# Output projection of a hybrid attention and retention block in seven half-size products

## Chip, cores and metric

One Trainium2 chip; the kernel runs on one core. The metric is device time in microseconds, the median of the runs of a kernel. The engines are named as the profile names them: PE is the Tensor engine (PEld its weight loads), DVE the Vector engine, ACT the Scalar engine, POOL GpSimd, SP the Sync engine, whose queue issues nearly all DMAs of this kernel.

## The reference

A block over 1024 tokens of width 2048, float32. One input projection (2048 to 5632 columns) feeds windowed attention (16 heads of 64, 4 key and value heads, a bias per head and distance, a sink) and bidirectional retention (8 heads, 64 keys, 128 values), each with a gate; the two branches are put side by side and go through the output projection, a residual and a last norm:

```python
h = rmsnorm(x, norm_w)
q_a, k_a, v_a, g_a, q_r, k_r, v_r, g_r = split(h @ w_in)
attn = rmsnorm(windowed_attention(q_a, k_a, v_a, sink, rel_bias), attn_out_norm_w) * silu(g_a)
ret = head_groupnorm(bidirectional_retention(rotary(q_r), rotary(k_r) / 8, v_r, ...), ret_gn_w) * silu(g_r)
mixed = concatenate([attn, ret], -1)          # 1024 x 2048
out = rmsnorm(x + mixed @ w_out, final_norm_w)
```

## The kernel before

Every operand of the two large projections is held as two float32r parts, high and low (`split`: a cast on ACT, then a subtraction on DVE or POOL), and a product is three matmuls: high by high, high by low, low by high.

Input projection: 22 units of 256 columns (`UNITS`), each over 16 rows of 128 of K (`k`), 8 weight tiles of 128 x 512 per unit. Normalised input lies in `hT`, 32 rows of 1024. Unit by unit the result is evicted (`evac`). The order of units is written out: keys, values and the first gates, then gates (`ga` of attention, `gr` of retention) between queries (`qa`), then pairs of `qk` and `vr` for retention, then the last gate (`gr`, 3).

Attention and retention run as generators beside the units: after each group of matmuls `point()` is called, which pumps one step of `jobs` (an attention job for each of four head groups g, later a retention job for each of four head pairs) at a pace per job, and at every second point one step of `aux` (gate post-processing, rotary, norms, bias rows, decay tables). `drain` runs a queue on until something is done. Each engine runs its own instructions in the order that the program comes to have; SP is one such queue for DMAs, and a DMA that waits there holds the ones behind it.

Weights: `w_load(i)` fetches the raw tile `wr` two tiles ahead, `w_split(i)` makes `wh` and `wl` one tile ahead. Raw tiles have two buffers; `wh` and `wl` have two each, and four once retention is over (`wide`). The subtraction is on POOL for the input weights and on DVE for the output weights.

An attention step takes 128 queries of a head: two matmuls of scores into `psS`, a DVE operation that adds the bias and finds the maximum (`P`, `nmx`), an exponential on ACT (L454), the normalisation on DVE (L462), transposes on PE into the one bank `psT` (L502), the copy of these to `PTh` on ACT (L513) and `PTl` on DVE, and the product with the values into `psO`.

Bias: `bias_rows` makes one row of 512 per head and copies it to 128 partitions through SBUF to the DRAM tensor `bd`, 16 heads in a row, a load `t<-br` and a store `bd<-t` each. Gates: `gate_post` takes a tanh on ACT (L362) and a multiply-add on DVE and stores to `gd`. Branch outputs go to the DRAM tensor `md`.

Output projection: two token halves (`hf`) by four column blocks of 512 (`cb`), each over 16 rows of K by four token blocks of 128, so 12 matmuls per weight tile. `mixed_row` fetches a row of `md`, multiplies in norms and gates where these are still missing, and splits it into `hT`: the first half during the last unit, the second during the first units of the projection. Banks `psM` and the set `psS`, `psT`, `psO` take turns. The last column block of the second half goes token block by token block, 48 matmuls each, from weights that were split ahead (on POOL).

## Time and profile before

| | us |
|---|---|
| median of 3 runs | 1580.43 (1579.05 to 1583.06) |
| profiled execution | 1581.46 |
| its span, first to last instruction | 1579.7 |
| mean granted TensorE clock | 0.994 of full speed |
| busy: PE | 1539.7 (97%) |
| busy: DVE | 798.9 (51%) |
| busy: ACT | 525.2 (33%) |
| busy: POOL | 414.1 (26%) |
| DMA, mean | 109 GB/s |

The stages in the profiled span: input units and setup to about 225 us, attention beside input units to about 800 us, retention beside input units to about 1240 us, the output projection from there. A busy time counts the time in which an engine has an instruction under way; matmuls overlap, so a busy PE is not one at its peak rate. An idle time is given with what ended it. A row of a group reads: line, engine, operation, output<-input by name, shapes, count, then busy us and mean ns of one, then the idle time just before these and what ended most of it.

### The profile page before, as it was taken

How to read it: one execution, taken by the hardware profiler on the slowest of the kernel's cores; microseconds unless marked ns; L12 is line 12 of the kernel's file. 1: busy time of each engine (PE TensorE's matmuls, PEld its weight loads, DVE VectorE, ACT ScalarE, POOL GpSimd, SP SyncE). 2: the span in 40 equal slices, each digit the busy share in tenths (PEclk: the TensorE clock that was granted, in tenths of full speed). 3: DMA queues.
4: the chain of work that ended last, by engine and by line, in shares of the span. 5: the costliest groups of instructions: out<-in, count | busy, mean ns of one | idle time of the engine just before them, and what ended most of it. 6: DMA issues, size and time to landing. Idle time of an engine off the chain costs nothing.

```text
span 1579.7 us, 22620 instructions
## 1 busy us (share of the span) xinstructions
PE 1539.7 (97%) x8338; PEld 1327.6 (84%) x8338; DVE 798.9 (51%) x1888; ACT 525.2 (33%) x1186; POOL 414.1 (26%) x435
## 2 busy tenths in 40 slices
PE   8979999999999999999999999999999999999997
PEld 6968888888888888888998998998988888888886
DVE  5511156644656478466534825735567463463323
ACT  5412145543554356456410111111123243433310
POOL 2212223332334334334331423323322000320000
PEclk9989999999999999999999999999999999999999
DMA  8774313131213123212231321312222565675423
GB/s 299 246 248 125 104 43 92 51 114 45 84 56 114 48 60 94 73 48 83 54 113 41 107 61 50 111 41 67 88 89 91 186 205 151 180 247 139 127 61 113
DMA packets 111020, 171.76 MB, mean 109 GB/s; under 512 B 17932, under 2 KB 39436, under 8 KB 110781
## 3 DMA queue, kind: packets, MB, share of 16 engines
q1 hardware_dynamic: 110908, 170.32, 35.3%
q8 instruction: 65, 1.06, 0.3%
q14 instruction: 47, 0.38, 0.1%
HBM read 138.26 MB, written 32.01 MB: 108 GB/s over the span
## 4 chain that ended last, share of the span: by engine, by line
PE 82%; DVE 8%; DMA 4%; issue 3%; ACT 1%; POOL 1%; SPq 0%; POOLq 0%; ACTq 0%; DVEq 0%
PE psM L817 14%; PE psM L818 14%; PE psM L819 14%; PE psM L811 3%; PE psM L812 3%; PE psM L810 3%; PE psM L900 3%; PE psM L901 3%; PE psM L899 3%; PE psT L502 2%; DMA t<-br 1%; DVE t L102 1%; PE psS L900 1%; PE psS L899 1%; PE psS L901 1%
## 5 line engine op out<-in xcount | busy, mean ns | idle before, releaser
L817 PE MATMUL psM<-hT,wh 128*128 128x512 f32 x1088 | 443.0, 407 | 14.9 <-ACT t L741 8.7
L819 PE MATMUL psM<-hT,wl 128*128 128x512 f32 x1088 | 425.9, 392 | 2.0 <-POOL wl L99 2.0
L818 PE MATMUL psM<-hT,wh 128*128 128x512 f32 x1088 | 426.2, 392 | 0.0
L99 POOL TENSOR_TENSOR wl<-wr,wh 128x512 fp32r<-128x512 f32 x176 | 234.5, 1333 | 583.7 <-ACT wh L105 570.7
L105 ACT CAST wh<-wr 128x512 fp32r<-128x512 f32 x288 | 178.5, 620 | 568.7 <-PE psM L818 226.4
L817 PEld LDWEIGHTS psM<-hT,wh 128*128 128x128 f32 x1088 | 205.7, 189 | 53.6 <-ACT t L741 8.9
L819 PEld LDWEIGHTS psM<-hT,wl 128*128 128x128 f32 x1088 | 204.9, 188 | 47.3 <-POOL wl L99 2.4
L818 PEld LDWEIGHTS psM<-hT,wh 128*128 128x128 f32 x1088 | 206.1, 189 | 37.5 <-DVE hT L102 0.7
L810 PE MATMUL psM<-wh,hT 128*128 128x256 f32 x640 | 183.5, 287 | 1.4 <-ACT wh L105 1.4
L811 PE MATMUL psM<-wl,hT 128*128 128x256 f32 x640 | 181.9, 284 | 2.4 <-POOL wl L99 2.4
L812 PE MATMUL psM<-wh,hT 128*128 128x256 f32 x640 | 181.8, 284 | 0.0
L99 DVE TENSOR_TENSOR wl<-wr,wh 128x512 fp32r<-128x512 f32 x112 | 84.1, 751 | 130.8 <-ACT wh L105 130.7
L811 PEld LDWEIGHTS psM<-wl,hT 128*128 128x128 f32 x640 | 123.4, 193 | 3.0 <-POOL wl L99 2.8
L810 PEld LDWEIGHTS psM<-wh,hT 128*128 128x128 f32 x640 | 123.5, 193 | 2.5 <-ACT wh L105 1.6
L812 PEld LDWEIGHTS psM<-wh,hT 128*128 128x128 f32 x640 | 123.4, 193 | 0.0
L450 DVE CUSTOM_DVE_ANT_0 P<-psS,bias,nsink 128x384 f32<-128x384 f32 (+1 forms) x128 | 74.3, 580 | 91.7 <-PE psS L444 91.3
L454 ACT ACTIVATE P<-P,nmx 128x384 f32<-128x384 f32 (+1 forms) x128 | 75.6, 590 | 92.1 <-DVE nmx L450 90.7
L900 PE MATMUL psM<-wl,hT 128*128 128x512 f32 x256 | 100.0, 391 | 0.6 <-DVE wl L99 0.5
L899 PE MATMUL psM<-wh,hT 128*128 128x512 f32 x256 | 100.0, 391 | 0.0
L901 PE MATMUL psM<-wh,hT 128*128 128x512 f32 x256 | 99.7, 389 | 0.0
L99 POOL TENSOR_TENSOR acc<-acc,sq 64x128 f32<-64x128 f32 x112 | 54.9, 490 | 156.2 <-ACT sq L483 148.1
L99 DVE TENSOR_TENSOR t<-psM,rb 128x512 f32<-128x512 f32 x64 | 42.2, 685 | 93.4 <-PE psM L819 93.2
(200 smaller groups left out, 2259.6 us busy)
## 6 DMA issues: line engine op xcount, KB each, us to landing
wr<-in_w_in SPq DMA_DIRECT2D x176, 256.0 KB, 2.7
wr<-in_w_out SPq DMA_DIRECT2D x112, 256.0 KB, 2.8
t<-in_x SPq DMA_DIRECT2D x16, 512.0 KB, 6.9
mr<-md SPq DMA_DIRECT2D x32, 256.0 KB, 3.0
xr<-in_x SPq DMA_DIRECT2D x32, 256.0 KB, 3.9
out<-y SPq DMA_DIRECT2D x32, 256.0 KB, 3.0
t<-in_xT SPq DMA_DIRECT2D x15, 512.0 KB, 5.8
gd<-t SPq DMA_DIRECT2D x28, 256.0 KB, 2.4
```

The lines of the kernel that those rows point to most:

```text
L99: eng.tensor_tensor(o, x, y, op)
L105: A.copy(o_hi, x)
L454: A.activation(x[:, :W], x[:, :W], AF.Exp, bias=nmx[:, c : c + 1], scale=-1.0, accum_out=sums[:, c : c + 1])
L810: T.matmul(po, hh[:, sl], wh[:, ws], start=first and z == 0, stop=False, skip_group_check=True)
L811: T.matmul(po, hh[:, sl], wl[:, ws], start=False, stop=False, skip_group_check=True)
L812: T.matmul(po, hl[:, sl], wh[:, ws], start=False, stop=last, skip_group_check=True)
L817: T.matmul(p, wh[:, ws], hh[:, sl], start=first, stop=False)
L818: T.matmul(p, wh[:, ws], hl[:, sl], start=False, stop=False)
L819: T.matmul(p, wl[:, ws], hh[:, sl], start=False, stop=last)
L899: T.matmul(p, mh, wh, start=(k == 0), stop=False)
L900: T.matmul(p, mh, wl, start=False, stop=False)
L901: T.matmul(p, ml, wh, start=False, stop=(k == NK - 1))
```

## The change

The output projection is cut into four problems: the two halves of K (f = 0 is the attention half, f = 1 the retention half) by the two halves of the columns (u). Each is a product of 1024 x 1024 by 1024 x 1024, taken as 2 x 2 blocks of 512 and computed in seven products of blocks (Strassen, in Winograd's form) in place of eight. A product p takes 4 rows of K by 4 token blocks by 3 matmuls. Its right operand is a block of `w_out` or one of four differences of blocks; its left operand a block of `mixed` or one of four combinations.

- `w_combine(f)` makes the weight differences: per f, u and row j, five loads, four DVE subtractions and four stores to DRAM (`wd`). It runs from a third queue, `slow`, which `point()` pumps at two of three points (at every point once retention is over), beside attention.
- `weigh_rows` multiplies attention's 16 half rows by norm weight and norm, DRAM to DRAM, and `combine_rows(f, j)` makes four combinations per j (two loads, one DVE operation, one store to `cd`), both beside retention, on two buffers `wc`. The last (f = 1, j = 3) and `gate_rows` follow in the first products.
- All 28 rows of the first half of K are loaded and split during the last unit (two per k); the 28 of the second half while the products run.
- PSUM: sums of products are read while they still grow (product 0 alone, then 0 + 2, and so on); each product's banks are evicted by an addition to one of four output blocks, 112 evictions of 128 x 512 in place of 32. The first seven products use one bank set, the others two in turn. Output sums of u = 1 go to DRAM (`yd`) and back between the halves of K.
- The weights' subtraction is on POOL for f = 0 and on DVE for f = 1.
- Bias rows: copies are made per group of four heads, from `slow`, one head at a time on the two `wc` buffers; groups 0 and 1 come in the first units, 2 and 3 later beside attention.
- Gates: one Silu on ACT, no DVE operation, and the factor 0.5 that went with tanh is dropped from `ew`.
- `t2` has four buffers in place of six. Keys and values are fetched straight into the tiles in which they are split.
- The last product goes token block by token block, 12 matmuls each; norms and stores of the second half of tokens follow block by block.

```diff
+ORDERS = {(0, 0): (1, 0, 2, 4, 5, 3, 6), (1, 1): (0, 1, 2, 3, 6, 4, 5)}
+W_OUT = [(f, u, p, j) for f in range(2) for u in range(2)
+    for p in ORDERS.get((f, u), (0, 1, 2, 3, 4, 6, 5)) for j in range(4)]
...
-            split(hi, lo, r, G if i < W_IN_TILES else V)
+            split(hi, lo, r, V if i >= W_IN_TILES and W_OUT[i - W_IN_TILES][0] else G)
+    def w_combine(f):
+        for u in range(2):
+            for j in range(4):
+                x, y = wc_(), wc_()
+                SP.dma_start(x, quarter(f, u, j, 1))
+                SP.dma_start(y, quarter(f, u, j, 0))
+                yield from pause(3)
+                tt(V, y, x, y, ALU.subtract)
+                yield
+                SP.dma_start(wd[f, u, 1, j], y)
...
+        if pt[0] % 3 or wide[0] is not None:
+            pump(slow, 1)
...
-        for h in range(16 + 1):
-            if h < 16:
-                reps[h] = t2()
-                b0 = br[h : h + 1, 0:512]
-                SP.dma_start(reps[h], bass.AP(tensor=b0.tensor, offset=b0.offset, ap=[[0, 128], [1, 512]]))
-            if h:
-                SP.dma_start(bd[h - 1], reps.pop(h - 1))
-            yield
+    def bias_copies(g):
+        for h in range(4 * g, 4 * g + 4):
+            r = wc_()
+            b0 = br[h : h + 1, 0:512]
+            SP.dma_start(r, bass.AP(tensor=b0.tensor, offset=b0.offset, ap=[[0, 128], [1, 512]]))
+            yield from pause(4)
+            SP.dma_start(bd[h], r)
+            yield
...
-            e = t2()
-            A.activation(e, g, AF.Tanh, scale=0.5)
-            yield
-            stt(V, g, e, 1.0, g, ALU.add, ALU.mult)
+            A.activation(g, g, AF.Silu)
+            yield
...
+    def combine_rows(f, j, tile):
+        if f:
+            yield lambda: ("ret", j) in done
+        for n, (x0, x1, op) in enumerate((
+            (q_mix(f, j, 2), q_mix(f, j, 3), ALU.add),
+            (q_mix(f, j, 0), q_mix(f, j, 2), ALU.subtract),
+            (cd[f, 1, j], q_mix(f, j, 0), ALU.subtract),
+            (q_mix(f, j, 1), cd[f, 0, j], ALU.subtract),
+        )):
+            x, y = tile(), tile()
+            SP.dma_start(x, x0)
+            SP.dma_start(y, x1)
+            yield from pause(3)
+            tt(V, y, x, y, op)
+            yield
+            SP.dma_start(cd[f, (1, 2, 0, 3)[n], j], y)
+            yield from pause(2 if n < 2 else 4)
...
+    slow.append((bias_rows(), 16))
+    slow.append((bias_copies(0), None))
+    slow.append((bias_copies(1), None))
+    slow.append((w_combine(0), None))
+    slow.append((bias_copies(2), None))
+    slow.append((bias_copies(3), None))
+    slow.append((w_combine(1), None))
+    def weighed():
+        yield lambda: "attn_norm" in done
+        yield from weigh_rows()
+        for j in range(4):
+            yield from combine_rows(0, j, wc_)
+    slow.append((weighed(), None))
+    for j in range(3):
+        slow.append((combine_rows(1, j, wc_), None))
...
+    into = {0: (0,), 1: (0,), 2: (1,), 3: (3,), 4: (3,), 5: (2,), 6: (1,)}
+    for n in range(nprod):
+        f, u, p, _ = W_OUT[4 * n]
+        if n < 7:
+            if p in (0, 1, 3):
+                X = Y = [psum("M", 4) for _ in range(4)]
+        elif p == 0:
+            sets = ([psum("M", 4) for _ in range(4)], [pS(), pS(), pT(), pO()])
+            X, Y = sets if (2 * f + u) % 2 == 0 else sets[::-1]
+        banks = Y if p in (1, 3, 6) else X
...
+        def products(j, t):
+            wh, wl = wsp[W_IN_TILES + 4 * n + j]
+            hh, hl = (H[p][:, j, 512 * z + 128 * t : 512 * z + 128 * t + 128] for z in range(2))
+            fresh = j == 0 and p in (0, 1, 3)
+            T.matmul(banks[t], hh, wh, start=fresh, stop=False, skip_group_check=True)
+            T.matmul(banks[t], hh, wl, start=False, stop=False, skip_group_check=True)
+            T.matmul(banks[t], hl, wh, start=False, stop=(j == 3), skip_group_check=True)
```

Three places in the order of instructions. First ACT, beside the second attention job, around the four gate operations of unit `ga` 2 (L362 before, L432 now; the exponentials are L454 before, L516 now). Before:

```order
L362 ACTIVATE t_501_3904<-t_478_3818 128x512
L479 COPY sq_3883<-psO_3875 64x256
L513 CAST PTh_3895<-psT_3891 128x3x128
L362 ACTIVATE t_505_3938<-t_482_3841 128x512
L454 ACTIVATE P_3872,sums_3870<-P_3872,nmx_3869 128x384
L483 ACTIVATE sq_3883<-u_3882 64x256
L362 ACTIVATE t_519_4000<-t_483_3846 128x512
L362 ACTIVATE t_520_4016<-t_484_3851 128x512
L513 CAST PTh_3895<-psT_3932 128x3x128
L454 ACTIVATE P_3923,sums_3870<-P_3923,nmx_3869 128x384
```

Now:

```order
L432 ACT_TABLE_LOAD
L432 ACTIVATE t_514_3994<-t_514_3994 128x512
L545 ACTIVATE sq_4036<-u_4035 64x256
L516 ACT_TABLE_LOAD
L516 ACTIVATE P_4076,sums_4023<-P_4076,nmx_4022 128x384
L519 ACTIVATE esk_4024<-esk_4024 128x2
L575 CAST PTh_4048<-psT_4085 128x3x128
L127 CAST wh_4103<-wr_4014 128x512
L432 ACT_TABLE_LOAD
L432 ACTIVATE t_515_3999<-t_515_3999 128x512
L516 ACT_TABLE_LOAD
L516 ACTIVATE P_4121,sums_4119<-P_4121,nmx_4118 128x256
```

Each gate operation now has a table load ahead of it, and so has the next exponential; 44 table loads stand in the program in place of one. Next SP, in unit 1, where the bias copies begin (`br` is the row of a head, `bd` its copy on 128 partitions). Before:

```order
L253 DMA t_58_774<-br 128x512
L255 DMA bd<-t_55_724 128x512
L255 DMA bd<-t_56_738 128x512
L255 DMA bd<-t_57_759 128x512
L253 DMA t_59_789<-br 128x512
L255 DMA bd<-t_58_774 128x512
L253 DMA t_60_804<-br 128x512
L143 DMA wr_811<-in_w_in 128x512
L255 DMA bd<-t_59_789 128x512
```

Now:

```order
L325 DMA wc_655<-br 128x512
L365 DMA dc_718<-in_ret_decay_bwd 64x4x1
L370 DMA jc_725<-in_jcol 128x2
L325 DMA wc_733<-br 128x512
L327 DMA bd<-wc_655 128x512
L172 DMA wr_804<-in_w_in 128x512
L425 DMA kd<-t_34_462 128x512
L327 DMA bd<-wc_733 128x512
L325 DMA wc_821<-br 128x512
L172 DMA wr_875<-in_w_in 128x512
L397 DMA t_66_819<-in_masks 128x512
L325 DMA wc_894<-br 128x512
```

Fewer copies stand between two weight loads, on two buffers in place of six, and key stores and the decay masks stand between them. Last SP beside retention (`wr` are weights, `so` and `md` retention's own rows, L803, L804 and L808 the combinations). Before:

```order
L143 DMA wr_10744<-in_w_in 128x512
L661 DMA md<-so_10676 128x512
L552 DMA qd_11424<-qdd 128x256
L656 DMA so_10971<-gd 128x512
L143 DMA wr_10805<-in_w_in 128x512
L661 DMA md<-so_10787 128x512
L550 DMA dt_11422<-dd 128x2x128
L143 DMA wr_10881<-in_w_in 128x512
```

Now:

```order
L808 DMA cd<-wc_10114 128x512
L172 DMA wr_10156<-in_w_in 128x512
L803 DMA wc_10201<-md 128x512
L804 DMA wc_10202<-cd 128x512
L172 DMA wr_10223<-in_w_in 128x512
L808 DMA cd<-wc_10202 128x512
L723 DMA md<-so_10166 128x512
L803 DMA wc_10327<-md 128x512
L612 DMA dt_10823<-dd 128x2x128
L804 DMA wc_10328<-md 128x512
L718 DMA so_10524<-gd 128x512
L808 DMA cd<-wc_10328 128x512
```

Between two weight loads there is now a combination's store, which waits for DVE, and the next one's loads, of which the second waits for that store.

More of the change, by code (lines that the diff above doesn't have):

```diff
@@ L855, in hybrid_block @@
             drain(aux, ("ga", i))
+            drain(slow, ("bias", i))
             jobs.append((attn_job(i, st, 16 * u + 17), None))
@@ new lines, in hybrid_block, with y_block, y_tile, e_load @@
+    for r in range(28):
+        if r in staged:
+            c_split(r)
+    E = {}
+    squares, yrows = {}, {}
+    def y_block(u, e, t):
+        tok, c0 = 512 * (e // 2) + 128 * t, 1024 * u + 512 * (e % 2)
+        return slice(tok, tok + 128), slice(c0, c0 + 512)
+    def y_tile():
+        return outp[0].tile([128, 512], F32, tag="yb", name=nm("yb"), bufs=8)
+    def e_load(f, u, e):
+        while stores:
+            SP.dma_start(*stores.popleft()[1:])
+        if f and not u:
+            return
+        if not f and not u:
+            if e == 0:
+                yrows[0] = hp.tile([128, 8, 512], F32, tag="h7", name="h7f", bufs=1)
+            elif e == 1:
+                pass
+            elif 1 not in yrows:
+                yrows[1] = outp[0].tile([128, 8, 512], F32, name="ya")
+        if f and e >= 2:
+            yrows[e] = h4(e - 2, F32)
+        for t in range(4):
+            if f and e >= 2:
+                d = yrows[e][:, t, 0:512]
+            elif u:
+                d = y_tile()
+            else:
+                d = yrows[e // 2][:, 4 * (e % 2) + t, :]
+            rows, cols = y_block(u, e, t)
+            SP.dma_start(d, yd[4 * e + t] if f else a["x"][rows, cols])
+            E[u, e, t] = d
@@ new lines, in hybrid_block, with finish @@
+    stores = deque()
+    weigh = deque()
+    def finish(e2, t):
+        v = small(1, "fv", 2)
+        V.tensor_reduce(v, squares[4 * e2 + t], mybir.AxisListType.X, ALU.add)
+        V.tensor_scalar(v, v, 1.0 / D, EPS, ALU.mult, ALU.add)
+        y, w = rsqrt_small(v, 1, "f", 2)
+        tt(V, y, y, w, ALU.mult)
+        for u, e in ((0, 2 * e2), (0, 2 * e2 + 1), (1, 2 * e2), (1, 2 * e2 + 1)):
+            d = E[u, e, t]
+            rows, cols = y_block(u, e, t)
+            if not u or e == 3:
+                A.activation(d, d, AF.Copy, scale=y)
+            else:
+                stt(V, d, d, y, fw[:, cols], ALU.mult, ALU.mult)
+            SP.dma_start(out[rows, cols], d)
```

440 lines of the change are left out of this document (259 added, 181 removed).

## Prediction

> **What bounds the kernel now.** I read the page first, then busy time by stretches, the groups of instructions, the Tensor engine's idle times, and the Scalar and Sync engines in order of time.
>
> ```profile
> span 1579.7 us, 22620 instructions
> PE 1539.7 (97%) x8338; PEld 1327.6 (84%) x8338; DVE 798.9 (51%) x1888; ACT 525.2 (33%) x1186; POOL 414.1 (26%) x435
> ```
>
> Stretches (length, then busy us and count of PE, PEld, DVE, ACT, POOL, granted clock, DMA share, GB/s) of attention and of the output projection:
>
> ```profile
> 300.00:500.00 200.00, 197.56 (x997) 167.81 (x996) 113.85 (x289) 93.41 (x242) 72.81 (x90) 1.00 0.28 81
> 500.00:700.00 200.00, 196.90 (x998) 165.35 (x997) 121.08 (x311) 98.60 (x261) 74.19 (x95) 1.00 0.24 66
> 1300.00:1400.00 100.00, 100.00 (x443) 82.70 (x442) 42.76 (x61) 41.25 (x79) 21.18 (x17) 1.00 0.58 172
> ```
>
> TensorE sets the end: in the projection it is never idle, in attention it idles under 2%. So matmuls removed are time removed, and whatever makes TensorE wait is time added. A matmul's own duration is not its price:
>
> ```profile
> L899 PE MATMUL psM<-wh,hT 128*128 128x512 f32 x256 | 100.0, 391 | 0.0
> L899 PE MATMUL psS<-wh,hT 128*128 128x512 f32 x96 | 37.4, 389 | 0.0
> L899 PE MATMUL psT<-wh,hT 128*128 128x512 f32 x48 | 18.7, 389 | 0.0
> L899 PE MATMUL psO<-wh,hT 128*128 128x512 f32 x48 | 18.7, 389 | 0.0
> L926 PE MATMUL psM<-hT 128*128 128x512 f32 x64 | 24.9, 389 | 0.0
> ...
> 1568.79 0.39 PE L927 MATMUL psM<-hT 128*128 128x512 f32 x1
> ...
> 1569.70 0.39 PE L928 MATMUL psM<-hT 128*128 128x512 f32 x1
> ```
>
> One lasts 0.39 us, but the last two rows are four starts apart, 0.2275 us each; 443 in 100 us are 0.2257. Neighbours overlap, so 0.2265 us is the price.
>
> **The sum, part by part.**
>
> 1. Matmuls. The groups above are one of three lines each: 3 x (256+96+48+48) + 3 x 64 = 1536. The change has 28 half-size products of 4 x 4 x 3 = 48: 1344. 192 fewer x 0.2265 = **-43.5 us**.
>
> 2. Bias copies. Before, all 16 heads' copies stand together in SP's queue, with the weight loads of unit 1 between them:
>
> ```profile
> 60.00:70.00 10.00, 10.00 (x86) 10.00 (x85) 4.64 (x10) 3.60 (x7) 4.21 (x3) 1.00 0.46 148
> 90.00:100.00 10.00, 7.69 (x59) 7.29 (x58) 0.00 (x0) 0.62 (x1) 1.26 (x1) 0.96 0.84 261
> 100.00:110.00 10.00, 5.67 (x38) 5.47 (x36) 0.00 (x0) 0.62 (x1) 1.26 (x1) 0.84 0.92 278
> 110.00:120.00 10.00, 5.63 (x14) 4.42 (x15) 1.75 (x4) 2.30 (x5) 1.28 (x1) 0.52 0.94 285
> ...
> 114.37 0.80 PE L817 MATMUL psM<-hT,wh 128*128 128x512 f32 x1 [8.70 <-ACT t L741]
> ...
> t<-br SPq DMA_DIRECT2D x16, 256.0 KB, 4.6
> bd<-t SPq DMA_DIRECT2D x16, 256.0 KB, 3.8
> ```
>
> At the rate of 86 small matmuls in 10 us, 90 to 110 us lose 75 x 0.116 = 8.7 us; 110 to 120 us lose 10 - 14 x 0.2265 = 6.8 us, with the granted clock down to 0.52. That is 15.5 us. Now eight heads stand there, on two buffers: four pairs, each a load and a store, 4.6 + 3.8 = 8.4 us, 34 us in a row, with five weight loads between them that TensorE wants in 27 us. The eviction of unit 1 also still waits for buffers that decay tiles hold behind those copies. So half of the stall stays: **-7 us** (0 to -15.5). The other eight heads' copies go beside attention, where DMA is busy a quarter of the time.
>
> 3. Activation tables. The gate was a tanh on ACT and a multiply-add on DVE; it becomes one Silu. The tanh needed no table of its own beside the exponentials: before, one ACT_TABLE_LOAD stands in the whole program, now 44. 40 of the new ones stand in six clusters inside attention (after each gate unit), in pairs around a Silu, each with attention's next exponential behind it in ACT's order. The one load in the trace, the gate's operation, two of the six 10 us windows around the gates (and their sum), and TensorE's slack:
>
> ```profile
> 0.72 1.28 ACT L772 ACT_TABLE_LOAD   x1 [0.72 <-PEq L1071]
> 2.02 0.19 ACT L772 COPY ones<-ones 128x1 f32<-128x1 f32 x1
> ...
> L362 ACT ACTIVATE t<-t 128x512 f32<-128x512 f32 x32 | 19.5, 629 | 4.1 <-DVE t L102 4.0
> ...
> 418.00:428.00 10.00, 10.00 (x52) 8.56 (x51) 9.66 (x21) 7.01 (x17) 4.23 (x4) 1.00 0.23 66
> 591.00:601.00 10.00, 9.72 (x52) 8.20 (x52) 9.91 (x27) 7.93 (x22) 5.07 (x6) 1.00 0.24 70
> sum 60.00, PE 59.19 PEld 50.39 DVE 56.96 ACT 42.97 POOL 24.93; mean PE 9.86 PEld 8.40 DVE 9.49 ACT 7.16 POOL 4.16
> ...
> 423.75 0.54 DVE L99 TENSOR_TENSOR PTl<-psT,PTh 128x384 fp32r<-128x384 f32 x1
> ...
> 425.70 0.49 PE L502 MATMUL psT<-ident,P 128*128 128x128 f32 x3
> 434.28 0.55 PE L502 MATMUL psT<-ident,P 128*128 128x128 f32 x3 [0.25 <-DVE PTl L99]
> ```
>
> 40 x 1.28 = 51.3 us more work on ACT, in windows where it is idle 60 - 43.0 = 17.0 us. Behind a late ACT stand the exponentials, the copy of the one transpose bank (PTh) and the casts of the weights; TensorE is in order and waits at the next transposes. It reaches them between 0 and 1.4 us after the bank is free (424.29 to 425.70; at 434.28 it waits already): 1.4 us of slack per cluster, 8.5 in all. 51.3 - 17.0 - 8.5 = 26; **+25 us**. Low end +8: each load before an exponential runs while that waits for its scores. High end +51: nothing is hidden. The Trainium skill speaks against the change here: "ScalarE: Activation LUTs", What ACT_TABLE_LOAD costs, gives 1283 ns for the load, as in the row above, and about 1380 ns of drain beside it, 2.66 us per switch. The trace shows no drain behind its one load (the copy starts as the load ends), and ahead of it ACT was idle, so that part no run here shows. By that price the term would be about +81 us.
>
> 4. Weight differences beside attention: 64 DVE subtractions, less 32 multiply-adds of the gate:
>
> ```profile
> L99 DVE TENSOR_TENSOR wl<-wr,wh 128x512 fp32r<-128x512 f32 x112 | 84.1, 751 | 130.8 <-ACT wh L105 130.7
> L102 DVE SCALAR_TENSOR_TENSOR t<-t,t 128x512 f32<-128x512 f32 x32 | 25.0, 805 | 2.1 <-ACT t L362 1.8
> ```
>
> 64 x 0.75 - 25 = +23 us on an engine with 40% idle; the cover is that idle time. Where it is gone (the 500 to 700 us stretch, TensorE idle 3.1 us, third attention job at the fastest pace) a 0.75 us operation falls on the path about four times: **+3 us** (0 to +10).
>
> 5. Row combinations beside retention. In SP's order, from weight tile 120 to 157 stand 16 weighings and 24 combinations on two buffers: load, DVE operation, store, and the next load into the stored buffer waits for the store. Between them stand the weight loads. From 830 to 1160 us:
>
> ```profile
> wr<-in_w_in SPq DMA_DIRECT2D x48, 256.0 KB, 2.7
> md<-so SPq DMA_DIRECT2D x12, 256.0 KB, 2.0
> so<-gd SPq DMA_DIRECT2D x10, 256.0 KB, 2.9
> ```
>
> A tile is 330 / 48 = 6.9 us, 37 tiles are 255 us: 6.4 us for each of 40 steps. A step takes 2.9 + 0.75 + 2.0 to 2.9 and some 0.3 of semaphores and issue: 5.9 to 6.9. SP's queue is about full, and a late store holds the weights behind it and DVE's next operations; two tiles loaded ahead absorb some 10 us. **+4 us** (0 to +20).
>
> 6. Output stage. The first seven products share one bank set, so each starts behind the eviction of the one before; bank 0 is finished 9 matmuls, 2.0 us, before the next product needs it, an eviction is 0.69 us, and DVE still has retention's work in three of them: 6 boundaries x 0.5. 56 weight tiles are split on POOL, 1.33 us against 0.75:
>
> ```profile
> L947 DVE TENSOR_TENSOR y<-psM,xr 128x512 f32<-128x512 f32 x19 | 12.6, 687 | 32.4 <-PE psM L928 15.4 <-DMA xr<-in_x 9.5 <-PE psM L901 7.5
> L99 POOL TENSOR_TENSOR wl<-wr,wh 128x512 fp32r<-128x512 f32 x176 | 234.5, 1333 | 583.7 <-ACT wh L105 570.7 <-PE psM L819 5.2 <-issue 2.5
> L105 ACT CAST wh<-wr 128x512 fp32r<-128x512 f32 x288 | 178.5, 620 | 568.7 <-PE psM L818 226.4 <-PE psM L812 135.3 <-DMA wr<-in_w_out 68.7
> wr<-in_w_out SPq DMA_DIRECT2D x112, 256.0 KB, 2.8
> ```
>
> 2.8 + 0.62 + 1.33 + 0.2 = 4.95 us on two raw buffers is 2.5 us per tile against 12 x 0.2265 = 2.7 on TensorE: hidden while loads stay below 3.3 us. 80 more evictions (55 us) and 24 more row splits lie in 305 us where DVE is 43% busy. **+6 us** (0 to +25).
>
> 7. End. The last product goes block by block, 12 matmuls (2.7 us) where 48 (10.9 us) stood, so three blocks' norms and stores crowd behind it; 9.6 us lie between the last matmul's end (1570.1) and the span's. **+2 us** (-2 to +8).
>
> -43.5 - 7 + 25 + 3 + 4 + 6 + 2 = -10.5 on a span of 1579.7: 1569.2. The profiled execution took 1581.46, 1.8 beyond its span and 1.0 over the median of 1580.43; against the median **1570 us**.
>
> **Rivals.**
>
> - Tables hidden. Each load that stands before a waiting exponential is free and the start stall goes wholly: +8 and -15.5 in place of +25 and -7: 1544.5. For it: ACT is 47% busy in attention. Against: the windows around the gates, where it is 72%.
> - Slower, by the switches. A load does not overlap the operation before it, which must leave first: 1.283 + 0.629 (a gate's operation) for each of 40, nothing hidden: 76.5 in place of 25: 1621.5. It decides from 36 us on (43.5 + 7 - 15 of the other terms). The page on ScalarE named above points the same way. Against: in the trace ACT operations follow within 0.1 us.
> - SP's queue full in retention. 7.1 us a step in place of 6.4: 40 x 0.7 = 28 in place of 4: 1594. For it: loads and stores there share SP with the rope tables and the retention's own rows.
> - Fewer matmuls but no faster projection: weight loads of 3.7 us make 2.93 us per tile, 56 x 0.21 = 12 us more: 1582. Against: 2.8 us at 172 GB/s.
>
> **How the numbers follow.** Forecast (1556 to 1585): 0.46; tables hidden: 0.20; switches: 0.17; SP: 0.12; feed: 0.05. 0.3% (4.7 us) is about what this kernel's runs tell from no change. Below 1575.7 lie the hidden case and 0.33 of the forecast's 0.46: faster 0.53; same 0.09 + 0.02 = 0.11; slower 0.36. The range leaves out the upper half of the switch case and the lower part of the hidden one: 1540 to 1618; the forecast's own is 1556 to 1585.
>
> **What would show it.** 1344 projection matmuls, still 0.227 us apart; TensorE's loss from 90 to 120 us near 8; 44 table loads of 1.28 us and, behind them, waits of TensorE on PTl of some 25 us in attention (none: hidden; 60 or more: switches); in retention, waits on weights or on retention's DVE results near 4; the projection 97% busy. The forecast is wrong if a load takes more than its row, or if SP's stores lag by more than the weights' lead.

## The result, and the profile after

The changed kernel takes 1630.38 us (median of 4 runs, 1628.26 to 1634.68) against 1580.62 us before (4 runs, 1579.05 to 1583.06): 1.0317 times as long, 95% interval 1.0292 to 1.0342. The forecast was 1570 us, 1540 to 1618: wrong in sign, and outside its range. (One later execution, of e13, was disturbed, 1677.8 us at a mean granted clock of 0.846; it is left out of that run's ratio, though not of its median, and its trace is not used.)

The head of the page of after, the page's instruction counts, and its busy time in stretches (columns as in the prediction), with retention's 900 to 1100 us:

```profile
span 1632.9 us, 23154 instructions
...
PE 1530.8 (94%) x8146; PEld 1303.9 (80%) x8146; DVE 890.5 (55%) x2000; ACT 594.5 (36%) x1254; POOL 467.3 (29%) x475
...
300.00:500.00 200.00, 193.22 (x958) 160.79 (x958) 117.11 (x293) 110.40 (x246) 68.44 (x85) 1.00 0.56 172
500.00:700.00 200.00, 193.10 (x959) 159.43 (x958) 122.01 (x300) 109.37 (x265) 71.31 (x90) 0.99 0.32 92
900.00:1000.00 100.00, 88.33 (x583) 80.60 (x582) 57.79 (x128) 10.28 (x18) 23.17 (x19) 0.91 0.55 177
1000.00:1100.00 100.00, 91.80 (x634) 84.22 (x633) 62.92 (x143) 12.61 (x22) 30.57 (x22) 0.99 0.54 175
1300.00:1400.00 100.00, 94.94 (x406) 76.03 (x405) 41.30 (x65) 25.54 (x43) 44.58 (x35) 0.98 0.73 235
```

The 192 matmuls are gone (8338 to 8146), and yet the span is 53 us longer. TensorE now waits in every stage, most beside retention, where before it hardly did:

```profile
900.00:1000.00 100.00, 99.90 (x656) 90.28 (x656) 48.25 (x126) 12.60 (x22) 29.18 (x25) 1.00 0.22 69
1000.00:1100.00 100.00, 98.99 (x662) 89.89 (x660) 49.02 (x124) 12.64 (x22) 30.02 (x25) 1.00 0.21 65
```

To set the stages beside each other I take the start of each unit's first eviction (the operations that read psM) from the timelines. Unit numbers count from 0: attention is read between units 4 and 14, retention between 14 and 21, the projection from unit 21 to TensorE's last end, and what follows is the end.

| stage (us) | before | after | difference |
|---|---|---|---|
| to unit 4 | 255.3 | 251.5 | -3.9 |
| attention | 567.9 | 592.9 | +25 |
| retention | 391.5 | 434.7 | +43 |
| projection | 355.3 | 337.1 | -18 |
| end | 9.6 | 16.8 | +7 |

The sum is +53. Read along TensorE instead: the gaps between its matmuls grew by 55 us over these stages (attention 6.1 to 21.6, retention 6.5 to 34.1, projection 0.6 to 16.9, start 17.3 to 12.7), the removed matmuls gave 43.5, and 35 us remain in which matmuls ran slower; the mean granted clock fell from 0.994 to 0.976, which is 30 us of such a span.

What TensorE waits for, and what DVE waits for, from the waits of the whole run, and in the last row the weights that TensorE waits for beside retention (840 to 1240 us); the numbers are total us, times, longest:

```profile
PE psM L952 <- DVE v L862: 22.7, 5, 5.9
PE psT L564 <- DVE PTl L121: 12.1, 14, 1.9
PE psO L537 <- DVE PTl L121: 8.9, 7, 3.6
...
PE psM L1178 <- ACT wh L127: 6.4, 3, 3.4
...
PE psM L1178 <- DVE ya L121: 4.0, 3, 2.0
...
DVE wc L121 <- DMA wc<-in_w_out: 98.2, 38, 6.5
DVE wc L121 <- DMA wc<-md: 55.5, 17, 5.9
...
DVE wc L121 <- DMA wc<-wd: 30.8, 11, 4.9
...
DVE wc L124 <- DMA wc<-md: 25.4, 8, 6.6
...
PE psM L946 <- POOL wl L121: 1.9, 2, 1.3
```

The pair to see is the rows of PE against the rows of DVE. TensorE waits for evictions and transposes of DVE (v, PTl), none of which the change touched; DVE waits 210 us for rows that the added operations (wc) still have to receive. Weights are not late beside retention: TensorE waits 1.9 us for them there. One of these places in the timelines of DVE, SP and TensorE, at the end of a retention unit (v is that unit's eviction, and the next unit's first matmul writes its bank):

```profile
960.11 0.69 DVE L121 TENSOR_TENSOR t<-t,sh 128x512 f32<-128x512 f32 x1
966.27 0.69 DVE L121 TENSOR_TENSOR wc<-wc,wc 128x512 f32<-128x512 f32 x1 [5.46 <-DMA wc<-md]
972.81 0.98 DVE L121 TENSOR_TENSOR wc<-wc,wc 128x512 f32<-128x512 f32 x1 [5.85 <-DMA wc<-md]
973.71 0.86 DVE L862 TENSOR_SCALAR v<-psM,rcol 128x256 f32<-128x256 f32 x2
...
966.99 0.32 SPq L808 DMA_DIRECT2D cd<-wc  x1
967.36 0.42 SPq L803 DMA_DIRECT2D wc<-cd  x1
967.83 0.44 SPq L172 DMA_DIRECT2D wr<-in_w_in  x1
969.07 0.32 SPq L804 DMA_DIRECT2D wc<-md  x1
...
968.67 0.28 PE L947 MATMUL psM<-wh,h7r 128*128 128x256 f32 x1
974.72 0.77 PE L952 MATMUL psM<-h0r,wh 128*128 128x512 f32 x1 [5.78 <-DVE v L862]
975.28 0.63 PE L953 MATMUL psM<-h0r,wh 128*128 128x512 f32 x1
975.71 0.63 PE L954 MATMUL psM<-h0r,wl 128*128 128x512 f32 x1
...
981.04 0.72 PE L952 MATMUL psM<-h0r,wh 128*128 128x512 f32 x1 [2.62 <-DVE v L862]
```

A step, from one combination to the next: operation 0.69, store issued at 966.99, the load into the stored buffer only at 969.07, and 3.7 us later the next operation starts (972.81). v, which was ready at 968.95, stands behind it on DVE and comes 4.8 us late. The 40 stores of the first chain stand from 840.03 to 1125.44 us, 7.3 us apart on average.

Retention's 43 us are not spread over the steps. From each unit's first eviction to the next unit's, units 14, 16, 18 and 20, the ones that v evicts, lose 11.6, 13.4, 7.8 and 7.6 us; the other three 1.7, 3.0 and -1.9. At units 16, 18 and 20 each late v stands right behind an operation that waited 4.9 to 5.9 us for its row, as above. At unit 14 none does: DVE has worked without such a wait since 839 us, and some of its operations are long, beside one of GpSimd (POOL):

```profile
843.00 2.73 POOL L121 TENSOR_TENSOR qs<-t,qd 64x1024 f32<-64x1024 f32 x1 [6.66 <-DVE t L121]
...
843.39 2.89 DVE L121 TENSOR_TENSOR sh<-sh,cs 128x512 f32<-128x512 f32 x1
...
850.68 1.65 DVE L862 TENSOR_SCALAR v<-psM,rcol 128x256 f32<-128x256 f32 x4
```

In attention the shape of unit 16 stands at a transpose split (PTl), behind a weight difference:

```profile
279.40 0.69 DVE L121 TENSOR_TENSOR wc<-wc,wc 128x512 f32<-128x512 f32 x1 [3.70 <-DMA wc<-in_w_out]
...
280.35 0.54 DVE L121 TENSOR_TENSOR PTl<-psT,PTh 128x384 fp32r<-128x384 f32 x1
...
280.94 0.55 PE L564 MATMUL psT<-ident,P 128*128 128x128 f32 x3 [1.79 <-DVE PTl L121]
```

### The profile page after: what moved, and what is told of

The parts are those of the page before. It is cut to its first block, busy times and chain, and to the rows that moved or that the text cites. A ratio compares the mean times of both kernels' runs of the same rounds, so it can differ in the third digit from the quotient of the medians.

```text
span 1632.9 us, 23154 instructions
## 1 busy us (share of the span) xinstructions
PE 1530.8 (94%) x8146; PEld 1303.9 (80%) x8146; DVE 890.5 (55%) x2000; ACT 594.5 (36%) x1254; POOL 467.3 (29%) x475
## 5 line engine op out<-in xcount | busy, mean ns | idle before, releaser
L121 POOL TENSOR_TENSOR wl<-wr,wh 128x512 fp32r<-128x512 f32 x232 | 314.3, 1356 | 709.3 <-ACT wh L127 687.4
L121 DVE TENSOR_TENSOR wc<-wc,wc 128x512 f32<-128x512 f32 x92 | 79.5, 864 | 223.3 <-DMA wc<-in_w_out 98.2
L516 ACT ACTIVATE P<-P,nmx 128x384 f32<-128x384 f32 (+1 forms) x128 | 75.6, 591 | 83.5 <-DVE nmx L512 82.3
L952 PE MATMUL psM<-h0r,wh 128*128 128x512 f32 x136 | 60.3, 445 | 31.7 <-DVE v L862 22.7
L121 DVE TENSOR_TENSOR PTl<-psT,PTh 128x384 fp32r<-128x384 f32 (+1 forms) x128 | 66.4, 519 | 26.7 <-ACT PTh L575 24.4
L564 PE MATMUL psT<-ident,P 128*128 128x128 f32 x352 | 61.2, 278 | 12.4 <-DVE PTl L121 12.1
L575 ACT CAST PTh<-psT 128x384 fp32r<-128x384 f32 (+1 forms) x128 | 57.7, 451 | 31.6 <-PE psT L564 29.5
L524 DVE TENSOR_SCALAR P<-P,sums 128x384 f32<-128x384 f32 (+1 forms) x128 | 60.2, 512 | 1.9
L952 PEld LDWEIGHTS psM<-h0r,wh 128*128 128x128 f32 x136 | 28.5, 210 | 40.5 <-issue 22.7
L953 PE MATMUL psM<-h0r,wh 128*128 128x512 f32 x136 | 57.8, 426 | 0.0
L954 PE MATMUL psM<-h0r,wl 128*128 128x512 f32 x136 | 56.9, 423 | 0.0
L952 PE MATMUL psM<-h7r,wh 128*128 128x512 f32 x136 | 56.0, 412 | 0.0
L952 PE MATMUL psM<-h4r,wh 128*128 128x512 f32 x136 | 55.5, 408 | 0.0
```

The source lines that it names most:

```text
L121: eng.tensor_tensor(o, x, y, op)
L516: A.activation(x[:, :W], x[:, :W], AF.Exp, bias=nmx[:, c : c + 1], scale=-1.0, accum_out=sums[:, c : c + 1])
L524: V.tensor_scalar(y[:, :W], y[:, :W], sums[:, cc : cc + 1], None, ALU.mult)
L564: T.transpose(p[:, 128 * i : 128 * i + 128], x[:, 128 * i : 128 * i + 128], ident)
L575: A.copy(hi[:, :nk, c, :], p3)
L952: T.matmul(p, wh[:, ws], hh[:, sl], start=first, stop=False)
```

## The experiments

Eighteen variants of the changed kernel, each timed beside the kernel before (1580.4 to 1582.3 us). Stage columns are us above the kernel before, read as in the table above; the projection is its length (before: 355.3). From profile to profile of kernels that do the same there, attention differs by up to 4 us either way, and retention stands 5 to 6 below after in e1, e3 and e8, which change nothing in it. The edits are shown by their main lines; what an edit no longer makes is replaced by plain rows or blocks where it is read.

| run | us | ratio [95%] | attention | retention | projection |
|---|---|---|---|---|---|
| after | 1630.4 | 1.0317 [1.0292, 1.0342] | +25 | +43 | 337.1 |
| e1_tanh | 1615.9 | 1.0224 [1.0207, 1.0241] | +11 | +37 | 339.4 |
| e2_norows | 1592.6 | 1.0076 [1.0061, 1.0091] | +25 | +1 | 338.6 |
| e3_noweights | 1609.7 | 1.0179 [1.0158, 1.0199] | +4 | +37 | 340.2 |
| e4_none | 1562.2 | 0.9877 [0.9852, 0.9902] | -5 | +1 | 341.8 |
| e5_pace | 1634.1 | 1.0333 [1.0308, 1.0357] | +25 | +43 | 337.2 |
| e6_pool | 1654.7 | 1.0465 [1.0437, 1.0494] | +34 | +41 | 337.2 |
| e7_batch | 1634.0 | 1.0317 [1.0273, 1.0361] | +23 | +43 | 338.1 |
| e8_noE | 1617.3 | 1.0229 [1.0198, 1.0260] | +24 | +38 | 325.9 |
| e9_noweigh | 1622.7 | 1.0261 [1.0231, 1.0292] | +35 | +21 | 337.9 |
| e10_three | 1623.7 | 1.0281 [1.0261, 1.0300] | +29 | +27 | 337.4 |
| e12_so1 | 1634.0 | 1.0362 [1.0320, 1.0404] | +21 | +42 | 337.9 |
| e11_bare | 1547.2 | 0.9792 [0.9774, 0.9810] | -5 | +3 | 323.9 |
| e13_nodve | 1602.6 | 1.0118 [1.0099, 1.0138] | | | |
| e14_dveonly | 1602.0 | 1.0121 [1.0106, 1.0136] | +23 | +12 | 336.8 |
| e15_queue | 1658.2 | 1.0480 [1.0464, 1.0496] | +27 | +57 | 342.9 |
| e16_nostore | 1634.8 | 1.0326 [1.0307, 1.0345] | +25 | +42 | 337.9 |
| e17_spread | 1631.2 | 1.0310 [1.0287, 1.0332] | +27 | +35 | 337.5 |
| e18_all | 1604.6 | 1.0132 [1.0112, 1.0153] | +7 | +29 | 340.3 |

**Which part costs.** Four runs take the added parts away, singly and together.

e1, no table switches:

```
-            A.activation(g, g, AF.Silu)
+            A.activation(g, g, AF.Tanh)
```

> The changed kernel with Tanh in place of Silu in the gates (the gate's value is then another function; no table switch is left, all else stays). Theory A (three causes: table switches in attention cost some 27 us, row combinations beside retention some 41 us, the projection some 20 us of its gain): 1630 - 27 = 1603 us. Rival B (the switches cost what the prediction's rival said, 76 us, and the rest follows from them): 1555 us. Rival C (the DMA volume, 260 MB for 172, is the cause and the tables are hidden): 1625 to 1635 us.

e2, no row work beside retention:

```
-    slow.append((weighed(), None))
-    for j in range(3):
-        slow.append((combine_rows(1, j, wc_), None))
```

> The changed kernel without the weighing and combining of rows beside retention (the rows of the first half of K and three quarters of the second are then read as they are). Theory A: retention takes its old time, 1630 - 41 = 1589 us, and TensorE's waits for the evictions of the value units (22.7 us) are gone. Rival B: at most the 4 us that the prediction gave this step, 1626 us. Rival C: a third of the extra DMA volume goes, some 17 us: 1613 us.

e3, no weight differences:

```
-    slow.append((w_combine(0), None))
-    slow.append((w_combine(1), None))
```

> The changed kernel without the weight differences (the products read plain blocks of the weights). Theory A: 64 DVE operations beside attention cost 3 to 5 us: 1625 us; table switches stay. Rival C: half of the extra DMA volume goes, some 25 us: 1605 us.

e4 makes all three edits.

> All three edits together: seven products, with no table switch, no weight differences and no rows beside retention. Theory A: the sum of the three, 1630 - 27 - 41 - 4 = 1558 us; if it were the full gain of 192 matmuls and of the start, 1580 - 43 - 6 = 1531 us. Rival B: 1550 us. Rival C: 1585 us.

The row work is worth 38 us of 1630 (and all of retention's loss: +43 to +1), the weight differences 21, the switches 14.5, all three 68. In attention the single effects overlap: 14 + 21 = 35 against 30 together. The kernel without them (e4) is 19 us faster than before, with another output. The switches are the least of the three. They are there in the trace of after:

```profile
L432 ACT ACT_TABLE_LOAD x22 | 28.2, 1283 | 7.2 <-DVE t L121 6.8
L516 ACT ACT_TABLE_LOAD x21 | 26.9, 1283 | 0.4
```

Without 43 of the 44 loads (e1) the kernel took 14.5 us less, 0.34 each: most of each load's 1.28 us was hidden. The Trainium skill ("ScalarE: Activation LUTs", What ACT_TABLE_LOAD costs) adds about 1380 ns of drain to each switch; the trace of after has no room for it: of the 43 loads behind another ACT operation 42 start within 0.02 us of its end, and behind 40 of them the next operation starts 0.01 us later. Putting the four Silus of a unit side by side (28 loads in place of 44) showed no gain, but the interval of e7, 7 us either way, is as wide as the 6 us that were sought:

```
+        for g in tiles:
+            A.activation(g, g, AF.Silu)
+        yield
         for b, g in enumerate(tiles):
...
-            A.activation(g, g, AF.Silu)
-            yield
```

> The changed kernel with the four Silus of a gate unit written next to each other: 28 table loads in place of 44. Leaving all switches out was worth 14.5 us for some 40 loads, 0.36 us each. Theory A: 16 fewer are worth 6 us: 1624 us. Rival: a longer block of ACT delays the transposes more at a time and gives it back: 1630 us.

**Why a row step costs a microsecond.** 44 steps cost 43 us. First the pause in weigh_rows between load and operation, 6 in place of 3:

```
-                yield from pause(3)
+                yield from pause(6)
```

> The changed kernel with six pumps in place of three between the loads of a weighed row and its DVE operation (16 rows; nothing else). Theory A1 (a row's chain of store, load and DVE operation is longer than the time that the program's order leaves for it, and DVE, in order, stands behind the load): the weighing has room, retention's loss falls from 43 us to 25 to 32: 1612 to 1620 us. Rival A2 (the loss is SP's queue as such, as many DMAs in it as before): no change, 1630 us.

Nothing changed, and the run tells less than it was made for: the 40 steps of the first chain stood as before (why the longer pause did not move them, this run does not show). Then the engine: all added subtractions and combinations on GpSimd, the 16 weighings still on DVE.

```
-            tt(V, y, x, y, op)
+            tt(G if tile is wc_ else V, y, x, y, op)
```

> The changed kernel with the weight differences and the row combinations on POOL in place of DVE (the weighing of 16 rows stays on DVE; same DMAs, same values). Theory A1: DVE's evictions and attention's DVE operations no longer stand behind loads; POOL stands there instead, where only the weights' second half (needed a tile later) queues: some 30 to 40 us less, 1590 to 1600 us. Rival A2 (SP's queue): 1625 to 1635 us. Rival A3 (the 1.3 us of a POOL subtraction and the weights' halves behind it make TensorE wait as long): no faster than 1620 us.

Worse by 24 us, and retention's loss the same 41. GpSimd splits the weights, and now those splits stand behind the late rows. TensorE's waits for v fall from 22.7 us to 5.8, those for the input weights' low half (wl) rise from 3.9 to 34.1; the largest group of waits in that run:

```profile
PE psM L954 <- POOL wl L121: 21.7, 18, 3.3
```

So whichever engine takes the operations holds up what stands behind them. Next fewer steps, more room, and the control for the room's price:

```
 e9   -        yield from weigh_rows()
 e10  -                n, r = wc_(), wc_()
      +                n, r = wx_(), wc_()
      -            x, y = tile(), tile()
      +            x, y = wx_() if tile is wc_ else tile(), tile()
 e10, e12
      -            so = rp.tile([128, 512], F32, tag="so", name=nm("so"), bufs=2)
      +            so = rp.tile([128, 512], F32, tag="so", name=nm("so"), bufs=1)
```

> Leaves out the 16 weighings of the forward rows (load, multiplication, store), so that the 24 combinations work on rows that were not weighed; the output is another one. 24 steps of the chain remain in the same two buffers. Theory 1 (each step of load, operation and store takes 7.3 us on the chip, but the fixed order of instructions leaves it less, so that every step costs its own difference): retention loses 24/40 of 42 us, about 25 in place of 42, and the kernel takes about 1614. Theory 2 (the chain as a whole is longer than the time in which it has to be done, 40 x 7.3 = 292 us of 330): 24 x 7.3 = 175 us fit with ease, retention loses less than 8 us and the kernel takes about 1592. Theory 3 (the DMA bytes of the steps load the queues): 16 weighings move 8 of 26 MB; about 1618.

> A third buffer beside retention: the first operand of a combination and the row vector of a weighing get a buffer of their own, so the two buffers in turn are free for the loaded row that is overwritten and stored; paid for by one buffer in place of two for retention's own rows (so). If the chain through two buffers is the cause, a step falls from 7.3 to about 5 us and retention loses under 15 us in place of 43: about 1602. If SP's queue is full in itself, or the loss is in DMA bytes, a step stays near 7 us: about 1630. If the single so buffer costs something of its own, the control with that alone shows it.

> The control for the third buffer: the changed kernel with one buffer in place of two for retention's own rows, and nothing else. If that buffer is of no account: 1630, within 3 us. If retention needs it: some us above, and the result of the third buffer has to be read against this one.

Without the weighings 12 of the 28 combinations stand far forward in attention (stores from 553 to 711 us), where the loss rose by 10, and retention's fell to 21: 31 us for 28 steps. That is 1.1 us a step, spread over 650 us, so the chain does not run out of time as a whole (theory 2); the microsecond is an average. With the third buffer (and a start of the weighings that asks for retention's buffers in place of attention's norm) most steps came some 5.4 us apart, and retention lost 27 in place of the control's 42: 15 us back, half of what was expected, and 10 in the whole kernel. Now one side of a step at a time:

```
 e13  -                stt(V, r, r, ew[:, kk : kk + 1], n, ALU.mult, ALU.mult)
      -            tt(V, y, x, y, op)
 e14  +        for n in range(16 + 28):
      +            yield from pause(3)
      +            tt(V, y, x, y, ALU.subtract)
 e15  -            SP.dma_start(x, x0)
      +            G.dma_start(x, x0)
 e16  -                SP.dma_start(row, r)
      -            SP.dma_start(cd[f, (1, 2, 0, 3)[n], j], y)
```

> Beside retention the weighings' and combinations' loads and stores stay, their DVE operations are left out (the loaded row is stored as it is; the output is another one). So far each of the 44 steps costs 1.0 us of retention, 42 in all. Theory A (DVE works in order, and a step's operation that waits for its late load keeps the evictions behind it): the loss falls below 8 us, the kernel takes about 1594. Theory B (SP works in order, and a load that waits for the store ahead of it keeps the weight loads behind it): SP's waits stay, the loss is 25 to 42, 1613 to 1630. Theory C (the bytes themselves): 42 and 1630.

> Only the 44 DVE operations stay, on two rows that are loaded once; all other loads and stores of the weighings and combinations are left out (the output is another one). They have no transfer to wait for. If DVE's time is what costs (44 x 0.75 = 33 us): retention loses 20 or more and the kernel takes 1610 or more. If theory A, B or C holds, DVE hides them: loss below 8, about 1594.

> The loads and stores of the weighings and combinations beside retention are issued by GpSimd in place of SP; nothing else is changed. Theory A: DVE waits for the same loads, no change, 1625 to 1635. Theory B: SP is free for the weights, the loss falls by 25 or more, 1605 or less (if GpSimd's weight splits, which then stand behind the waiting stores, do not take its place). Theory C: 1630.

> The stores of the weighings and combinations beside retention are left out, the loads and DVE operations stay (the combinations read plain rows, so the output is another one). A load then waits for no store, only for the DVE operation two steps ahead. Theory A and B, if the way over the store is what makes the loads late: the loss falls below 12, 1600 or less. Theory C: two thirds of the bytes stay, 28 of 42, about 1616. If loads come late without the stores too, it stays near 1630.

All transfers without the operations: 1.0118 times before, 1601 us. All operations without their transfers: 1.0121, 1602. With neither (e2) it is 1.0076, so either half alone costs some 7 us; together they cost 38. So it is not the bytes (theory C), and for the most part not DVE's time, but an operation that waits in order for its transfer (theory A). Unit by unit e14 divides the loss: unit 14 loses the same 11.7 us as in after, with no row to wait for, and units 16, 18 and 20 lose 0.0, 0.0 and 0.6. So the wait for rows is the cause at these three, 29 us, and DVE's added time at unit 14; e14's 12 us in retention miss the 8 that were expected.

SP's queue (theory B) is spoken against by the 1.9 us that TensorE waits for weights beside retention. e13 does not separate it, since SP's stores then wait for no DVE operation either, and e15 only in part: with GpSimd issuing, the steps were no shorter and DVE waited longer, but GpSimd's weight splits stood behind waiting stores, as the expectation for theory B had allowed:

```profile
POOL cd L808 <- DVE wc L121: 87.6, 22, 6.4
...
DVE wc L121 <- DMA wc<-md: 71.7, 17, 7.7
```

e16 missed what I expected of theory A. Without stores the steps stood closer (4.2 to 5 us for half of them), and DVE waited for its loads all the same:

```profile
DVE wc L121 <- DMA wc<-md: 70.3, 23, 4.7
```

The last two runs tie the order instead of asking for it by a pause. Each added operation is tied behind the DVE operation written before it, with pause 4; e18 adds e10's third buffer, and ties the weight differences too, with a pause of 6 for the second half.

```
+            with tc.issue_after(lastv[0]):
+                tt(V, y, x, y, op)
-                yield from pause(3)
+                yield from pause(4)
 e18  -                yield from pause(3)
      +                yield from pause(6 if f else 3)
```

> The changed kernel complete, with two things different: each DVE operation of the weighings and combinations beside retention is tied behind the DVE operation written before it, so that it can't be put ahead, and the written pause between load and operation is 4 in place of 3. In the order of instructions the 44 steps now stand over weight tiles 122 to 176 (1.25 tiles, some 8.5 us each) in place of 122 to 158 and 168 to 171. Theory A (an operation on DVE waits for its load because the steps stand closer than the 7.3 us they take): the steps now have their time, DVE's waits and retention's loss fall from 43 to below 20: about 1607. If a step costs its microsecond however far apart the steps stand: 1630 as before.

> The same ties and pause, with the third buffer of e10 beside retention, and the same tie for the subtractions of the weight differences beside attention, the second 32 of which now stand over weight tiles 60 to 110 in place of 54 to 82; complete. Theory A: retention's loss falls below 12 (steps of 5.5 us with 8.5 us of room), attention's from 25 to about 17, the kernel takes about 1590, still behind the kernel before, since the projection and the end keep their losses. If spacing is no help: 1620 or more.

In attention, where tie and longer pause came together (e18), it works as theory A says: 25 to 7 us of loss, and DVE's wait for these rows is halved (98.2 in 38 waits to the row below), TensorE's for PTl in psT 12.1 to 6.7. e17, with attention's order untouched, keeps +27 there.

```profile
DVE wc L123 <- DMA wc<-in_w_out: 51.8, 17, 6.7
...
PE psM L967 <- DVE v L877: 14.4, 3, 6.4
```

In retention the ties gave back only 8 (e17, hardly more than the 5 to 6 by which e1, e3 and e8 differ there, and the kernel's time is that of after), and with the third buffer 14 (e18): a miss. What is left stands where it stood, at the end of each unit that v evicts (8.2 to 9.4 us at each of four in e17), as the second row shows. In e18's timeline the one with the 6.4 us wait (v at 949.62) has no wait for a row ahead of v, but a DVE that has been at work since 936 us on rope, the retention's own rows and two combinations, with two gaps of 0.7 us (for rope's tables); before, it had been idle 19 us when this v came. So there DVE's arrears, not one late row, make v late, as at unit 14 of after. Part of them are long operations: GpSimd is at work from 941.67 to 948.54 us, and beside it the operation that makes qs takes 2.95 us, against 1.21 at 1194.54 us in after, and two rotary ones 1.74 and 1.64, where they take 0.69 alone. What else makes the arrears, the runs don't settle.

**The projection.** e8 leaves out the loads of residual and intermediate blocks and their stores; e11 does that and all of e4.

```
-            SP.dma_start(d, yd[4 * e + t] if f else a["x"][rows, cols])
+            fresh_e.add((u, e, t))
-            if u:
-                stores.append((pt[0] + 3, yd[4 * e + t], d))
```

> The changed kernel without the loads of the residual into the output blocks and without the store and reload of the sums between the halves of K (64 DMAs of 256 KB fewer in the projection; a block's first eviction is then a copy, and its values lack these parts). Theory O1 (the projection's lost 25 us are bursts of such DMAs in front of weights and of evictions that wait for them): 18 to 25 us less, 1606 to 1612 us. Rival O2 (the first seven products' one bank set, evictions on a busy DVE): 5 us less at most, 1625 us.

> The seven products bare: Tanh in place of Silu, no weight differences, no weighings and combinations beside retention, and no loads or stores of residual and intermediate blocks around the output stage; the products take plain weights and plain rows, so the output is another one. If the 43.5 us that the removed matmuls are worth are there, and the rest of the loss was in those four parts: attention and retention within 2 us of the kernel before, the projection about 355 - 43.5 = 312 us from the end of unit 21 to the last matmul, the end 5 us longer than before: about 1535. If the seven products have a loss of their own (evictions between products on shared banks, weight splits on GpSimd): the projection above 325 us and about 1550.

e11 is 33 us faster than before, 0.9792. Its products run at full pace, nineteen of them between these rows (10.88 us each, 48 x 0.2267):

```profile
1292.34 0.39 PE L1175 MATMUL psS<-wh,h0r 128*128 128x512 f32 x1
...
1499.06 0.39 PE L1175 MATMUL psS<-wh,h4r 128*128 128x512 f32 x1
```

So the 43.5 us are real; 12 of them stay lost even there (355.3 - 43.5 = 311.8 against 323.9), in the first seven products and the last two. There TensorE waits 5.7 us for evictions (ya, h7f) from the banks that the first seven products share, and 4.1 us at the last. Of the 25 lost in after, 11 come back without the block transfers alone (337.1 to 325.9). The place where they are lost, in after (SP, ACT and TensorE):

```profile
1403.99 1.06 SPq L1043 DMA_DIRECT2D yb<-in_x  x2
1405.12 0.89 SPq L172 DMA_DIRECT2D wr<-wd  x2
1406.05 2.14 SPq L842 DMA_DIRECT2D mr<-cd  x4
...
1410.40 1.30 ACT L127 CAST wh<-wr 128x512 fp32r<-128x512 f32 x2 [5.04 <-DMA wr<-wd]
...
1411.07 0.68 PE L1178 MATMUL psM<-wh,h3r 128*128 128x512 f32 x1 [3.42 <-ACT wh L127]
```

Weight loads are issued behind a batch of block loads and land some 5 us later, while a weight tile gives TensorE 2.7 us of work. The longer end (16.0 to 16.8 in every variant, against 9.6) stays in e11 too, so it does not come from the block transfers; the last product's form is what is left, which no run changes.

## Why the prediction was wrong

1. Matmuls, -43.5: right; e11's products stand 0.2267 us per matmul.
2. Bias copies, -7: about right; -7.1 at unit 2, -3.9 by unit 4.
3. Tables, +25: too high. e1 puts them at 14.5; the rival with 76 is refuted (a load takes 1.31 us between two operations of ACT in the trace, not 1.912). Hidden wholly they were not.
4. Weight differences, +3 (0 to +10): 21 by e3. The two terms' sum, 28, is near attention's 25, by accident of two errors. The failing sentence is "the cover is that idle time": DVE is idle there, but while it waits for a row, what stands behind that operation waits too (PTl above, behind a wait of 3.70 us).
5. Row combinations, +4 (0 to +20): 43. This step decided the result. The 6.4 us that a step has, and the 5.9 to 6.9 it takes, were put side by side as if a queue could absorb the difference. Measured, a step takes 7.3, of which DVE stands waiting up to 5.9, and the evictions behind it pay: 29 of the 43 at units 16, 18 and 20. Another 11.6, at unit 14, are DVE's added time (e14), for which the term had nothing. The rival "SP's queue full" had the step nearly right (7.1), but the wrong queue and too low a price (28).
6. Output, +6 (0 to +25): 25, at its upper end. The feed was taken as hidden "while loads stay below 3.3 us"; what broke it was the issue order for 11 of the 25 (e8), with block loads ahead of weights; of the rest, waits for evictions from the shared banks are a part, where the term had 3.
7. End, +2 (-2 to +8): +7.

Missing altogether was that an idle TensorE comes back slow. After the wait of 968.9 to 974.7 above, the starts are 0.43 us apart (975.28, 975.71) in place of 0.2265. The clock that this trace records is either 1.00 or 0.50. Stretches of after around the wait, cut where it changes (the granted clock is the third number from the right):

```profile
960.00:968.90 8.90, 8.90 (x75) 8.74 (x73) 1.46 (x3) 1.46 (x3) 1.82 (x1) 1.00 0.71 242
971.00:977.70 6.70, 2.98 (x7) 2.43 (x8) 1.76 (x3) 0.62 (x1) 1.26 (x1) 0.50 0.51 151
977.80:981.10 3.30, 0.68 (x4) 0.25 (x2) 1.48 (x3) 0.00 (x0) 0.00 (x0) 1.00 0.17 64
981.20:984.50 3.30, 3.30 (x8) 2.58 (x9) 0.00 (x0) 0.00 (x0) 0.00 (x0) 0.50 0.86 264
985.00:1005.00 20.00, 20.00 (x106) 16.59 (x105) 11.88 (x26) 1.86 (x3) 4.20 (x5) 1.00 0.44 137
```

Over the run, 55 us more of gaps went with 35 us of slower matmuls: a microsecond of waiting cost 1.6 on average. Between variants it is about the same: e2 has 25 us fewer gaps than after, and its TensorE ends 42 us earlier, e18 17 and 29. The half clock accounts for about 21 of the 35 us: TensorE is busy for 51.3 us at 0.50 in after and for 8.7 before, and half of such time is lost. The other 14 are not explained. The Trainium skill's "TensorE: Matmul & The Clock Gate", What's actually happening, has the array at half clock by default, released after about 3.4 us of work; the trace agrees with 2.98 and 3.30 us of work in the two stretches at 0.50.

## What to carry to other kernels

Work put "beside" another stage on an engine that runs in order is hidden only if its operand has landed when its turn comes: cost it by load latency and buffer turnaround (here 7.3 us for load, operation and store through two buffers), and look up in the order of instructions which eviction stands behind it. Test such a suspicion with two runs, the transfers without the operation and the operation without the transfers; where both are cheap and the pair is dear, it is the wait. Look at the loss unit by unit in both: a part that stays without the transfers is the engine's own time. Tied order with a longer pause gave back 18 of 25 us in attention, ties and a third buffer only 14 of 43 in retention; each microsecond of TensorE's wait saved here is worth about 1.6.

## What the hardware showed that was not expected

- After waits of 5.8 and 2.6 us TensorE worked at half clock (0.50) for some 3 us each time.
- A table load of 1.283 us cost 0.34 us of the whole; the next ACT operation started 0.01 us behind it in 40 of 43 places.
- DVE's additions, subtractions and products of two 128 x 512 operands in SBUF took 0.69 us at most in retention where no GpSimd operation ran beside them (57 in after, 31 before), and 1.16 us on average where one did (36; before 20, 1.01 us).
- Moving the row transfers' issue from SP to GpSimd made the kernel 28 us slower (1630.4 to 1658.2), and moving the operations there 24.
- None of the complete variants beats the kernel before; the best, e18, is at 1.0132 times its time.
